# The first input tile alone at the head of SyncE's queue, one scaling piece on VectorE, and two small orders in layer 1

## The chip, the cores and the metric

The kernel runs on one core of a Trainium2 chip. The metric is the device time of one execution in microseconds; the median of several runs is compared. Five engines work side by side and meet through semaphores: TensorE (PE, with its weight loads PEld), VectorE (DVE), ScalarE (ACT), GpSimd (POOL) and SyncE (SP), which only issues transfers here. ACT and POOL issue transfers too; the queues of SP, ACT and POOL feed the same DMA engines.

## The reference

Two sequences of 512 tokens of width 1024 go through two layers and a final norm. Layer 0 mixes by a Fourier transform in 8 groups of 128 features, layer 1 by attention (8 heads, 2 key heads). Behind each stands a squared-ReLU MLP of width 4096. All is float32.

```python
def rms_norm(x, g):
    y = x32 * lax.rsqrt(jnp.mean(x32 * x32, axis=-1, keepdims=True) + EPS)
    return (y * g.astype(jnp.float32)).astype(x.dtype)

def fourier_mix(h, w_out):
    hg = h.astype(jnp.float32).reshape(B, S, N_FGROUPS, F_GROUP)
    f = jnp.fft.fft2(hg, axes=(1, 3), norm="ortho").real
    return f.reshape(B, S, D_MODEL) @ w_out

def sq_relu_mlp(h, w_up, w_down):
    a = jnp.maximum(h @ w_up, 0)
    return (a * a) @ w_down

for i in range(DEPTH):
    if i % N_MIXERS == 0:
        x = x + fourier_mix(rms_norm(x, fourier_norm[j]), fourier_w_out[j])
    else:
        x = x + gqa_attention(rms_norm(x, attn_norm[j]), ...)
    x = x + sq_relu_mlp(rms_norm(x, mlp_norm[i]), mlp_w_up[i], mlp_w_down[i])
return rms_norm(x, final_norm)
```

## The kernel before

**Numbers.** Nearly every float32 product is made of three products of halves: an operand is split into a high part (`split`: a cast on ACT, L86) and a low part (a subtraction on DVE, L87), and PE adds high x high, high x low and low x high in PSUM (`mm3`, `product`). The first transforms use plain float32.

**The head.** `begin()` starts the transfers. `g` is the Fourier norm's gain, 128 x 8 numbers (L377, on SP's queue). `load_x(0, t)` brings tile t of sequence 0, 128 tokens x 1024 (L352); tile 0 goes through ACT's queue, tiles 1 to 3 through SP's. `exact_table(4)`, `(5)` and `(6)` bring the tables of cosines and sines (L366, SP). SP's queue thus holds, in this order: g, tile 1, table 4, tiles 2 and 3, tables 5 and 6, and the Nyquist weights (L731). PE meanwhile runs `idle`, matmuls of 256 columns on a tile of ones, whose result nobody reads (L622): 12 of them, then 8 transposes that spread g over the partitions (L392), then 20 more.

All engines follow the written order here (`manual_schedule`). `f0 = Front(0, 0)` handles tiles 0 and 1. For each tile, ACT squares and sums (`squares`, L445) and POOL takes the inverse root (`root`, L449 and L450). Then, for tile 0, DVE multiplies by the gain in two halves, straight from the PSUM of g's transposes (`gain`, L459), adds the two halves (`plus`, L463) and subtracts them (`minus`, L472). `scale_both(0)` multiplies by the inverse root on ACT (L484) in four pieces: the sum's first 128 columns, its other 384, a short extract (128 x 40) for the Nyquist row, and the difference (128 x 512). The first piece is what the first matmul of the sequence transform reads (`exact_even`, L547), together with the first 258 columns of table 4. Then come `exact_nyq` (L554), which reads the extract, and `exact_odd` (L550), which reads the difference. Tile 1 goes the same way, and tiles 2 and 3 follow through `f1`, whose two tiles `combine` joins (L493 to L495).

**The MLP, first product.** The matrices are multiplied by a seven-product scheme on blocks of two by two. In `first_product` pairs of hidden blocks p = 0 to 15 run; for the first eight, the two products of a pair that go into its first row (`first`, `second`) come ahead of all others. `first` accumulates in a PSUM bank, and ACT copies the bank (L1081, `blocks.copied`). `second` goes on accumulating in the same bank, so it must wait for the copy. When it is done, ACT applies ReLU (L1062) and the square (L1063, `squared`). Here PE's order is in part written and in part the planner's; ACT's and DVE's order come from the planner, which takes `behind(x, y)` as an order between two instructions, without a wait. In layer 1, `behind(pairs[p - 1].squared, blocks.copied)` puts the square of one pair behind the copy of the next, for p from 4.

**The MLP, second product.** `second_product` walks over groups of 4, 4, 2 and 4 pairs in layer 1. For each group and each of four output columns m there is a step (`Sums`, five products) with a row (`Row`, two products) of the group that comes next. The row's first product is added to a common part on DVE (`add_e`, L1269, `r.added`). The operands were spilled to memory; `hook` brings the next group's back when it is time, and `put` splits each into two halves; `puts` holds their low parts. Where a step's rows have n = 2 and four low parts arose in the step, `behind(puts[1], rows[0].added)` puts the second low part behind the row's add. PE's order is written in this loop; the planner sets the others'.

Of the kernel before, what the change touches and what calls it, by code (L numbers as in the profile page):

```python
# [44 lines left out]
def trunk_kernel(ctx, tc, x_in, xt_in, y_out, tables, rope, gfour, gcol, grow, gfin,  # L45
# [298 lines left out]
    def load_x(q, t, queue=nc.sync):  # L344
        if (q, t) == (0, 0):
            wide = wp.tile([P, 2 * D], F32, tag="w", name=nm("w"))
            nc.vector.memset(wide[:, D : D + 1], (EPS * D) ** 0.5)
            xa[q, t] = wide[:, :D]
            xa[q, t, "eps"] = wide[:, : D + 1], wide[:, D + 4 :].bitcast(BF16)[:, : D + 1]
        else:  # L350
            xa[q, t] = slot([P, D], F32)
        return queue.dma_start(xa[q, t], x_in[q][t * P : (t + 1) * P, :])  # L352
# [8 lines left out]
        tabs[k] = slot([P, D], F32R)  # L361
        nc.gpsimd.dma_start(tabs[k][:, : tables[k].shape[-1]], tables[k])

    def exact_table(k):
        t = slot([P, D], F32)
        nc.sync.dma_start(t[:, : tables[k].shape[-1]], tables[k])  # L366
        exact.append(t)

    def w_pair(src, n, a):
        b = slot([P, D], F32)  # L370
# [3 lines left out]

    def begin():
        gr, g = slot([P, D], F32), cons.tile([P, KC], F32, name="g")
        nc.sync.dma_start(g, gfour)  # L377
        load_x(0, 0, nc.scalar)
        load_x(0, 1)
        exact_table(4)  # L380
        for t in range(2, 4):
            load_x(0, t)
        exact_table(5)
        exact_table(6)
        nc.scalar.preload_act_table_set("natural_log_exp_and_others")
        idle(ps(), 12)
        halves = []
        for i in range(2):
            o = ps()
            for k in range(4):  # L390
                c = 4 * i + k
                nc.tensor.transpose(o[:, k * P : (k + 1) * P], g[:, c : c + 1].broadcast_to([P, P]), ident)  # L392
            halves.append(o)
        return gr, halves
# [36 lines left out]
    class Front:  # L431
# [46 lines left out]
        def scale_both(self, i):  # L478
            if i == 0:
                self.n = exact[0][:, 772:852].rearrange("p (i a b) -> p i a b", i=2, a=5)  # L480
            p, m = self.p[i], self.m[i]
            first = ((p[:, :P], p[:, :P]), (p[:, P:], p[:, P:])) if i == 0 else ((p, p),)
            for out, x in first + ((self.n[:, i], eights(m)), (m, m)):
                nc.scalar.activation(out, x, AF.Copy, scale=self.r[:, i : i + 1])  # L484
                yield
            parts.append((self.p[i], self.m[i], self.n[:, i]))

# [131 lines left out]
    def idle(o, n):  # L619

        for _ in range(n):
            nc.tensor.matmul(o[:, :256], filler, filler.unsqueeze(1).broadcast_to([P, 2, P]), start=True, stop=True)  # L622
# [174 lines left out]
    with tc.manual_schedule(engines={ET.PE, ET.Activation, ET.DVE, ET.Pool, ET.SP}):  # L797
# [4 lines left out]
        ftX, pickX = exact[2][:, :256], exact[2][:, 256:334]  # L802
        f0, f1, wn = Front(0, 0), Front(0, 1), FoldNyq()
        wn.load()
        idle(ps(), 20)
        for i in range(2):
            f0.squares(i)
            f0.root(i)
# [244 lines left out]
    def first_product(l, blocks, rows, ahead, head=iter(())):  # L1053
# [122 lines left out]
        for p in range(AHEAD):  # L1176
            if p == late + 1:
                blocks.spread(1)
            pair = pairs[p]
            if p < len(rows):  # L1180
                pair.row = rows[p]
            else:
                pair.load()
                pair.split_row()
                if p < 6 and wo_added:
                    behind(pair.made[1], wo_added[0])
                if p == 4 and not l:
                    for x, y in zip(pair.made, blocks.r[1].made):
                        behind(x, y)
            with tc.manual_schedule(engines={ET.PE}) if p < 3 else nullcontext():  # L1190
                pair.first()
                if l and p > 3:
                    behind(pairs[p - 1].squared, blocks.copied)
                if p == 1:
                    blocks.split_sums(1)
                next(head, None)
                if p == 1:
                    pairs[0].second()
                if p == 2 == late:
                    blocks.root(1)  # L1200
                if p > 0:
                    pair.second()
                if p == 1 == late:
                    blocks.root(1)
            if p > 3:
                for _ in range(3):
                    next(todo)
            if p == 5:
                pairs[0].load_sums()
                pairs[0].sums_13()  # L1210
                pairs[0].sum_2()
            if p == 6:
                pairs[0].split_23()
# [36 lines left out]
    def second_product(l, blocks, rows, late=lambda: None, ready=lambda m: None, head=iter(())):  # L1250
# [214 lines left out]
        for k, (rows, sums) in enumerate(items):  # L1465
            nrows, nsums = items[k + 1] if k + 1 < len(items) else ([], None)
            end = sums.m if sums.g == len(GROUPS[l]) - 1 else -1
            if end in (0, 2):
                late()
            puts.clear()  # L1470
            with tc.manual_schedule(engines={ET.PE}):
                for r in rows:
                    r.first()
                    if r.m == 3:
                        change("b11", r.g)
                for r in nrows:
                    r.load()
                hook()
                for i, op in enumerate(("t1", "t3", "t2", "b22", "t4")):
                    sums.go(i)  # L1480
                    if sums.m == 3:
                        change(op, sums.g)
                    if i == 0 and nsums:
                        nsums.load()
                    if i == 1:
                        for r in rows:
                            r.second()
                            if r.m == 3:
                                change("b21", r.g)
                        if end == 1:  # L1490
                            late()
                            late()
                        hook()
                        for r in nrows:
                            r.split()
                    if i == 4 and nsums:
                        nsums.split_3()
                    hook()
                    if k == 0 and i in (2, 4):
                        change(ROW[i // 4], 0)  # L1500
                    if i == 2 and nsums:
                        x = nsums.sum_23()
                        if sums.n < nsums.n:
                            for r in rows:
                                behind(x[0], r.added)
                            for y in puts[2:]:
                                behind(y, x[1])
                        nsums.split_12()
                    if i == 3 and nsums:
                        nsums.sum_4()  # L1510
                        nsums.split_4()
            if rows and rows[0].n == 2 and len(puts) == 4:
                behind(puts[1], rows[0].added)
            for r in rows:
                finish(r.m)
            finish(sums.m)
# [728 lines left out]
```

## Time and profile before

| what | value |
|---|---|
| median of 3 runs | 1661.48 us (1661.46 to 1661.52) |
| the profiled execution | 1660.31 us |
| its span, first to last instruction | 1658.5 us |
| PE busy, matmuls | 1651.5 us, 7762 instructions |
| DVE, ACT, POOL busy | 1265.0, 878.3, 394.1 us |
| granted TensorE clock, mean | 0.999 |

The span is shorter than the execution by what lies around the first and the last instruction. Times in a timeline count from the span's start. A row of the timeline has start and duration in us, the engine, the line of the kernel, the operation, out<-in, and how many instructions were merged; brackets give the engine's idle time before it and what ended it. ACTq and SPq are the issuing parts of ACT and SP. A duration of merged matmuls reaches to the modelled end of the last one, so groups overlap a little.

### The profile page before, as it was taken

How to read it: one execution, taken by the hardware profiler on the slowest of the kernel's cores; microseconds unless marked ns; L12 is line 12 of the kernel's file. 1: busy time of each engine (PE TensorE's matmuls, PEld its weight loads, DVE VectorE, ACT ScalarE, POOL GpSimd, SP SyncE). 2: the span in 40 equal slices, each digit the busy share in tenths (PEclk: the TensorE clock that was granted, in tenths of full speed). 3: DMA queues.
4: the chain of work that ended last, by engine and by line, in shares of the span. 5: the costliest groups of instructions: out<-in, count | busy, mean ns of one | idle time of the engine just before them, and what ended most of it. 6: DMA issues, size and time to landing. Idle time of an engine off the chain costs nothing.

```text
span 1658.5 us, 22101 instructions
## 1 busy us (share of the span) xinstructions
PE 1651.5 (100%) x7762; PEld 1378.5 (83%) x7762; DVE 1265.0 (76%) x1797; ACT 878.3 (53%) x1551; POOL 394.1 (24%) x377
## 2 busy tenths in 40 slices
PE   9999999999999999999999999999999999999998
PEld 8988888888888888888888888888888888888887
DVE  8898785557886779868788888877855487878875
ACT  7776454446243425447688856554554552433335
POOL 5311443222000001325454303004422220000002
PEclk9999999999999999999999999999999999999999
DMA  9843554459775757425501146335544696756632
GB/s 313 241 172 108 196 210 165 146 193 371 229 237 172 246 180 228 177 66 199 166 1 39 65 175 231 127 108 180 201 149 168 226 366 200 233 163 221 186 114 103
DMA packets 121904, 301.43 MB, mean 182 GB/s; under 512 B 12312, under 2 KB 13720, under 8 KB 121792
## 3 DMA queue, kind: packets, MB, share of 16 engines
q1 hardware_dynamic: 98864, 253.66, 43.8%
q0 software_dynamic: 8528, 20.01, 5.7%
q10 hardware_dynamic: 14400, 26.35, 4.2%
q8 instruction: 61, 1.00, 0.2%
q14 instruction: 51, 0.42, 0.1%
HBM read 217.07 MB, written 82.38 MB: 181 GB/s over the span
## 4 chain that ended last, share of the span: by engine, by line
PE 98%; DVE 1%; issue 0%; ACT 0%; DMA 0%; POOL 0%; POOLq 0%; DVEq 0%; ACTq 0%
PE ps L1046 76%; PE ps L83 6%; PE ps L81 6%; PE ps L82 6%; PE ps L1657 2%; PE ps L1636 0%; PE ps L550 0%; PE ps L547 0%; DVE u L2002 0%; DMA g<-gfour 0%; PE ps L217 0%; PE ps L622 0%; PE ps L760 0%; PE ps L1626 0%; PE ps L587 0%
## 5 line engine op out<-in xcount | busy, mean ns | idle before, releaser
L1046 PE MATMUL ps<-u,w 128*128 128x512 f32 x4920 | 1124.6, 389 | 0.0
L1046 PEld LDWEIGHTS ps<-u,w 128*128 128x128 f32 x4920 | 922.7, 188 | 193.8 <-ACT u L1081 1.9
L86 ACT CAST w<-raw 128x1024 fp32r<-128x1024 f32 (+1 forms) x215 | 212.4, 993 | 309.6 <-PE ps L1046 235.9
L87 DVE TENSOR_TENSOR w<-raw,w 128x1024 fp32r<-128x1024 f32 (+1 forms) x215 | 249.3, 1164 | 66.6 <-ACT w L86 62.6
L86 ACT CAST u<-u 128x1024 fp32r<-128x1024 f32 (+1 forms) x140 | 140.7, 1046 | 84.9 <-PE ps L1046 37.4
L87 DVE TENSOR_TENSOR u<-u,u 128x1024 fp32r<-128x1024 f32 (+1 forms) x140 | 168.9, 1233 | 21.6 <-ACT u L86 20.7
L1046 PE MATMUL ps<-u,u 128*128 128x512 f32 x624 | 148.6, 389 | 0.0
L1296 POOL DMA_DIRECT2D raw<-w_sum x32 | 28.1, 879 | 468.5 <-DMA raw<-w_sum 167.6
L1166 POOL TENSOR_TENSOR u<-u 128x512 f32<-128x512 f32 x28 | 37.8, 1351 | 427.6 <-ACT u L1063 427.6
L1269 DVE TENSOR_TENSOR u<-ps,u 128x512 f32<-128x512 f32 x160 | 109.4, 685 | 36.8 <-PE ps L1046 34.0
L1046 PEld LDWEIGHTS ps<-u,u 128*128 128x128 f32 x624 | 117.1, 188 | 24.3
L81 PE MATMUL ps<-u,u 128*128 128x512 f32 (+2 forms) x342 | 129.0, 379 | 0.0
L83 PE MATMUL ps<-u,u 128*128 128x512 f32 (+2 forms) x342 | 124.5, 364 | 0.0
L82 PE MATMUL ps<-u,u 128*128 128x512 f32 (+2 forms) x342 | 124.2, 363 | 0.0
L177 POOL TENSOR_TENSOR t<-t,t 128x512 f32<-128x512 f32 (+1 forms) x47 | 67.5, 1441 | 187.2 <-ACT t L171 163.2
L1062 ACT ACTIVATE t<-t 128x512 f32<-128x512 f32 x64 | 40.5, 632 | 111.4 <-DVE t L1135 101.4
L87 DVE TENSOR_TENSOR u<-ps,u 128x512 fp32r<-128x512 f32 (+3 forms) x112 | 68.1, 635 | 7.3 <-ACT u L86 6.9
L83 PEld LDWEIGHTS ps<-u,u 128*128 128x128 f32 x342 | 64.3, 188 | 10.5 <-DVE u L87 0.4
L82 PEld LDWEIGHTS ps<-u,u 128*128 128x128 f32 x342 | 64.6, 189 | 8.5 <-DVE u L87 0.7
L81 PEld LDWEIGHTS ps<-u,u 128*128 128x128 f32 x342 | 64.7, 189 | 7.8
L1122 DVE TENSOR_TENSOR t<-ps,u 128x512 f32<-128x512 f32 x32 | 22.0, 687 | 60.9 <-PE ps L1046 50.3
L86 ACT CAST u<-ps 128x512 fp32r<-128x512 f32 (+3 forms) x112 | 59.4, 558 | 9.6 <-PE ps L1657 7.6
(270 smaller groups left out, 2013.3 us busy)
## 6 DMA issues: line engine op xcount, KB each, us to landing
raw<-w_up SPq DMA_DIRECT2D x80, 512.0 KB, 4.6
u<-spill_t SPq DMA_DIRECT2D x60, 512.0 KB, 7.0
raw<-w_sum SPq DMA_DIRECT2D x56, 512.0 KB, 5.6
u<-spill_b SPq DMA_DIRECT2D x45, 512.0 KB, 6.4
spill_t<-u SPq DMA_DIRECT2D x84, 256.0 KB, 2.0
spill_b<-t ACTq DMA_DIRECT2D x60, 256.0 KB, 4.2
raw<-w_row SPq DMA_DIRECT2D x28, 512.0 KB, 4.8
park<-u SPq DMA_DIRECT2D x24, 512.0 KB, 3.9
```

The source lines that it names most:

```text
L81: nc.tensor.matmul(out, lh, rh, start=first, stop=False)
L82: nc.tensor.matmul(out, lh, rl, start=False, stop=False)
L83: nc.tensor.matmul(out, ll, rh, start=False, stop=last)
L86: hi = nc.scalar.copy(dst_hi, src)
L87: return hi, eng.tensor_sub(dst_lo, src, f32(dst_hi))
L177: nc.gpsimd.tensor_add(acc[q][:, :n], acc[q][:, :n], s[:, :n])
L1046: nc.tensor.matmul(o, w[x][:, sl], h[k][y], start=first and k + i == 0, stop=k == n - 1 and i == 2, skip_group_check=not first)
L1062: nc.scalar.activation(t, src, AF.Relu)
L1166: eng.tensor_sub(t[:, 0], b12, b11)
L1269: return nc.vector.tensor_add(x, o, x)
L1296: nc.gpsimd.dma_start(s[:, 1], w[:, 3], accum_op=ALU.add)
L1657: nc.tensor.transpose(pt[:, t * P : (t + 1) * P], probs[t][:, sc * P : (sc + 1) * P], ident)
```

## The change

In the head, g moves to ACT's queue. Tile 0 moves to the head of SP's. Table 4 is brought in two transfers: its first 258 columns right behind tile 0, the rest behind tile 1. `exact_table` becomes a generator that issues one transfer at each step. The fillers ahead of the transposes go from 12 to 10, those behind them from 20 to 21. The first of tile 0's four scaling pieces moves from ACT to DVE, as a `tensor_scalar` with the same per-partition factor; the other pieces stay on ACT. In layer 1, the order of square and copy in the first product begins with pair 3 instead of 4. In the second product, all four low parts go behind the row's add, instead of the second one alone.

```diff
-    def exact_table(k):
+    def exact_table(k, cuts=()):
         t = slot([P, D], F32)
-        nc.sync.dma_start(t[:, : tables[k].shape[-1]], tables[k])
         exact.append(t)
+        edges = [0, *cuts, tables[k].shape[-1]]
+        for c0, c1 in zip(edges, edges[1:]):
+            nc.sync.dma_start(t[:, c0:c1], tables[k][:, c0:c1])
+            yield
...
-        nc.sync.dma_start(g, gfour)
-        load_x(0, 0, nc.scalar)
+        nc.scalar.dma_start(g, gfour)
+        load_x(0, 0)
+        pieces = exact_table(4, (258,))
+        next(pieces)
         load_x(0, 1)
-        exact_table(4)
+        for _ in pieces:
+            pass
         for t in range(2, 4):
             load_x(0, t)
-        exact_table(5)
-        exact_table(6)
+        for k in (5, 6):
+            for _ in exact_table(k):
+                pass
         nc.scalar.preload_act_table_set("natural_log_exp_and_others")
-        idle(ps(), 12)
+        idle(ps(), 10)
...
-            for out, x in first + ((self.n[:, i], eights(m)), (m, m)):
-                nc.scalar.activation(out, x, AF.Copy, scale=self.r[:, i : i + 1])
+            for j, (out, x) in enumerate(first + ((self.n[:, i], eights(m)), (m, m))):
+                if i == j == 0:
+                    nc.vector.tensor_scalar(out, x, self.r[:, :1], None, ALU.mult)
+                else:
+                    nc.scalar.activation(out, x, AF.Copy, scale=self.r[:, i : i + 1])
                 yield
...
-        idle(ps(), 20)
+        idle(ps(), 21)
...
-                if l and p > 3:
+                if l and p > 2:
                     behind(pairs[p - 1].squared, blocks.copied)
...
             if rows and rows[0].n == 2 and len(puts) == 4:
-                behind(puts[1], rows[0].added)
+                for y in puts:
+                    behind(y, rows[0].added)
```

## The prediction

> **What bounds the kernel now.** I read the page first, its busy shares and its chain of waits.
>
> ```profile
> span 1658.5 us, 22101 instructions
> PE 1651.5 (100%) x7762; PEld 1378.5 (83%) x7762; DVE 1265.0 (76%) x1797; ACT 878.3 (53%) x1551; POOL 394.1 (24%) x377
> PE 98%; DVE 1%; issue 0%; ACT 0%; DMA 0%; POOL 0%; POOLq 0%; DVEq 0%; ACTq 0%
> ```
>
> PE is busy for all but 7.0 of the 1658.5 us, and 98% of the chain is PE's own work. So an edit on another engine counts only where PE waits for it, and an edit of PE's own fillers counts directly, because PE has no later pause in which a late start could be made good. Next I read the timeline of the first 30 us, where most of the edits lie. Its columns are start, duration, engine, line, operation, and in brackets the idle time before it and what ended that.
>
> ```profile
> 0.72 0.41 ACTq L352 DMA_DIRECT2D w<-x  x1
> 0.73 0.39 SPq L377 DMA_DIRECT2D g<-gfour  x1
> 0.94 0.17 DVE L408 MEMSET u<- 128x128 f32 x1
> 1.16 2.93 PE L622 MATMUL ps<-u 128*128 128x256 f32 x12 [1.16 <-DVE w L347]
> 1.17 0.42 SPq L352 DMA_DIRECT2D u<-x  x1
> 4.32 1.23 PE L392 MATMUL ps<-ident,g 128*128 128x128 f32 x8 [0.23 <-DMA g<-gfour]
> 4.89 1.06 ACT L445 ACTIVATE w<-w 128x1025 bf16<-128x1025 f32 x1 [2.44 <-DMA w<-x]
> 5.16 1.28 DVE L459 TENSOR_TENSOR u<-w,ps 128x512 f32<-128x512 f32 x2 [3.99 <-PE ps L392]
> 5.31 2.64 PE L622 MATMUL ps<-u 128*128 128x256 f32 x20
> 6.12 1.06 ACT L445 ACTIVATE t<-u 128x1024 bf16<-128x1024 f32 x1
> 6.20 0.57 POOL L450 TENSOR_TENSOR s<-s,half 128x1 f32<-128x1 f32 x1 [3.72 <-ACT w L445]
> 6.47 0.69 DVE L463 TENSOR_TENSOR t<-u 128x512 f32<-128x512 f32 x1
> 7.08 0.68 DVE L472 TENSOR_TENSOR t<-u 128x512 f32<-128x512 f32 x1
> 7.26 0.91 ACT L484 ACTIVATE t<-t,s 128x128 f32<-128x128 f32 x2
> 7.79 2.00 PE L547 MATMUL ps<-u,t 128*128 128x257 f32 x8
> 8.46 0.72 ACT L484 ACTIVATE t<-t,s 128x512 f32<-128x512 f32 x1
> ...
> 16.25 0.81 DVE L495 SCALAR_TENSOR_TENSOR t<-t,s,t 128x512 f32<-128x512 f32 x1
> ...
> 17.51 0.59 PE L547 MATMUL ps<-u,t 128*128 128x257 f32 x2
> ```
>
> The reader is to see three strands that meet at 7.79, where the first real matmul (L547) begins. PE: 12 fillers, a 0.23 us wait for g, eight transposes of g, 20 fillers. DVE: it waits 3.99 us, not for the input tile but for the transposes (at 5.16), and then works through two gains, `plus` and `minus` without a pause. ACT: from 4.89 it squares tile 0, then tile 1, and only at 7.26 gets to the scaling piece that L547 reads. L547 starts when the last filler has been issued and the piece is ready, both at about the same time.
>
> **The change part by part: the head.** The fillers first. Twelve took 2.93 us, 0.244 each, so ten end at 1.16 + 2.44 = 3.60 instead of 4.09. The transposes cannot start before g has landed. g goes from SP's queue, issued at 0.73, to ACT's, issued at 0.72: 0.01 us apart. The next view is the DMA queues from 3.8 to 4.4 us (q10 is ACT's, q1 SP's).
>
> ```profile
> q10 hardware_dynamic: 50, 0.16, 65.6%
> q1 hardware_dynamic: 25, 0.09, 36.7%
> ```
>
> Here both queues are served side by side: while the last 0.16 MB of tile 0 move, 0.09 MB of SP's transfers move too. In front of SP's queue, with only g's 128 x 8 x 4 bytes beside it, tile 0 no longer shares this stretch. Two thirds of the engines' packets were its own, so some 0.2 of these 0.6 us are gained: it lands at 4.7 instead of 4.89. g stays one of two heads of queue issued at the same moment, so I take its landing as unchanged, with 0.2 us either way as a bound. The wait before the transposes then grows from 0.23 to 0.72 us: the two fillers taken away become idle time, and the transposes start at 4.32 as now. The added filler (2.64 / 20 = 0.13) has PE ready at 7.92 instead of 7.79.
>
> DVE is released by the transposes, so it starts at 5.16 as now, and an earlier tile 0 gives it nothing. `minus` ends at 7.76. Behind it comes the new operation, the 128x128 scaling. No DVE row shows this operation; the bounds are 0.17 (the 128x128 memset) and 0.41 (a two-input 128x256 pass, quoted below). I take 0.25, nearer the row of the same shape, and it ends at about 7.97, allowing 0.04 for the overlap that DVE's rows show (`minus` starts 0.08 before `plus` ends). L547 then starts at 8.0, **0.2 us later than now**.
>
> On ACT one piece goes away (two of them took 0.91). Against that, tile 1 now stands behind the first 258 columns of the table, 128 x 258 x 4 bytes = 0.13 MB, which is 0.3 us at the 0.25 MB in 0.6 us of the two rows above. The square of tile 1 moves from 6.12 to about 6.4, and the later scalings (the row at 8.46) end at about 9.3 instead of 9.18. They are read only after L547's eight matmuls, which end at 9.79 now and 0.2 later then, so this costs nothing; without that cover it would cost 0.1. What is late next is DVE, which has 0.25 us more in front of all its later work: at its end, the row at 16.25 finishes at 17.06 and L547 reads it at 17.51. The slack of 0.45 covers the 0.25, the more so as PE is later itself. The one added DMA issue (0.42 on SP) and tile 0's own move past g lie in front of transfers that stand in line anyway. The order of SP's bytes is otherwise as before, and the first part of the table lands sooner.
>
> The bounds of the head: if g landed by 3.60, PE would reach L547 at 3.60 + 0.99 (4.32 to 5.31) + 21 x 0.132 = 7.36, but DVE could not start before tile 0 at 4.7, and its chain of 2.6 us plus 0.25 gives 7.5: a gain of 0.3. If g landed 0.2 later, the loss would be 0.4.
>
> **The change in layer 1: the square.** The edit at line 1192 lets `behind` begin with pair 3 instead of pair 4. These are ACT's rows around pairs 3 and 4, then the weight loads' rows and their group of waits from 1040 to 1630 us.
>
> ```profile
> 1051.75 1.04 ACT L86 CAST w<-raw 128x1024 fp32r<-128x1024 f32 x1
> 1052.69 0.63 ACT L1063 ACTIVATE u<-u 128x512 f32<-128x512 f32 x1
> 1053.22 0.57 ACT L1081 COPY u<-ps 128x512 f32<-128x512 f32 x1
> ...
> 1057.44 1.04 ACT L86 CAST w<-raw 128x1024 fp32r<-128x1024 f32 x1
> 1058.53 0.59 ACT L1081 COPY u<-ps 128x512 f32<-128x512 f32 x1
> ```
>
> ```profile
> 1053.85 5.13 PEld L1046 LDWEIGHTS ps<-u,w 128*128 128x128 f32 x23 [0.33 <-ACT u L1081]
> 1059.17 0.99 PEld L1046 LDWEIGHTS ps<-u,w 128*128 128x128 f32 x5 [0.20 <-ACT u L1081]
> ```
>
> ```profile
> PEld ps L1046 <- ACT u L1081: 1.0, 4, 0.3
> ```
>
> PE accumulates pair 3's second product onto the bank that the copy (L1081) reads, so it waits for the copy. At pair 3 the square (L1063) stands between the cast and the copy; at pair 4 it does not. Put behind the copy, the square lets it start at 1052.69 instead of 1053.22, 0.53 earlier, which is more than the 0.33 that PE waited. The wait goes. Its worth is between 0 (if it hid behind matmuls in flight) and 0.33; I take **0.25 gained**, since such loads stand a little apart anyway. The square itself ends 0.5 later, in front of a store that nobody near awaits. Pair 4's 0.20 stays.
>
> **The four low parts.** The edit at line 1513 acts where a step's rows have n = 2 and four low parts are made: the step whose seven products of six matmuls end where PE's row at 1515.62 begins. At 0.227 us each (twelve from 1515.62 to 1518.34) these 42 take 9.5 us, so it starts at 1506.1. DVE's rows and PE's:
>
> ```profile
> 1505.28 1.22 DVE L87 TENSOR_TENSOR u<-u,u 128x1024 fp32r<-128x1024 f32 x1
> 1507.01 1.22 DVE L87 TENSOR_TENSOR u<-u,u 128x1024 fp32r<-128x1024 f32 x1
> 1508.74 0.68 DVE L1269 TENSOR_TENSOR t<-ps,t 128x512 f32<-128x512 f32 x1
> 1509.34 1.22 DVE L87 TENSOR_TENSOR u<-u,u 128x1024 fp32r<-128x1024 f32 x1
> 1511.07 1.21 DVE L87 TENSOR_TENSOR u<-u,u 128x1024 fp32r<-128x1024 f32 x1
> ...
> 1514.61 0.41 DVE L1344 TENSOR_TENSOR raw<-raw,raw 128x256 f32<-128x256 f32 x1
> ...
> 1517.61 0.68 DVE L87 TENSOR_TENSOR u<-raw,u 128x512 fp32r<-128x512 f32 x1
> ```
>
> ```profile
> 1515.62 2.88 PE L1046 MATMUL ps<-u,w 128*128 128x512 f32 x12
> 1518.34 2.88 PE L1046 MATMUL ps<-u,u 128*128 128x512 f32 x12
> ```
>
> Two low parts now run ahead of the row's add at 1508.74; afterwards all four run behind it. The row's product ends at 1506.1 + 6 x 0.227 = 1507.5, so the add can come at about 1507.7, and DVE stands idle for some 1.2 us before it. The lows follow from 1508.3, each with an add between, and end by about 1515. Their first reader is PE at 1515.62, which wants the second pair only one product and two sums later. Everything queued behind them moves by about 1.2 us: the low at 1517.61 would end at 1519.5 instead of 1518.29. It is read in the second product after 1518.34, six matmuls later (1519.7), at its third matmul (1520.2). The cover is 0.7 us. So the price is **0**, with bounds of 0 and about 0.5 if two more operations slip in front. It gains nothing either: the group of waits above holds nothing from this place.
>
> **The sum.** +0.2 - 0.25 + 0 = -0.05 us. The profiled execution took 1660.31 us, 1.81 around its span of 1658.5; the sum makes it 1660.26. The median of the runs, 1661.48, is 1.17 above the profiled one, so the forecast is **1661.4 us**, no change.
>
> **The rivals.** (1) *The clock stays low longer: slower.* The fillers went from 0.244 us each (the twelve) to 0.132 (the twenty): PE's pace doubles somewhere in the transposes, after some 3.5 us of nearly unbroken work. With 0.72 us of idle in that stretch instead of 0.23, the doubling may be refused. Then the 21 fillers cost up to 21 x 0.244 = 5.1 instead of 2.8, or, if the low pace lasts another 3.5 us, half of that is lost: +1.8, so 1663.2. It decides from the first such stretch; beyond 0.2% it takes two. For it speaks that idle time triples; against it that 0.23 did no harm and 80% of the stretch is still busy. [...]
>
> (2) *g lands earlier in ACT's queue.* Then the head gains up to 0.3 instead of losing 0.2, and with the square it is -0.55: 1660.9. For it: on ACT's queue g stands beside the tile from the first packet. Against: it did so on SP's.
>
> (3) *The low parts come too late.* DVE's idle 1.2 us is not caught up and PE waits at 1520: +0.5 to 1.2 on the forecast, 1662.2. For it: the first five DVE rows above alone take 5.6 of the 7.0 us from 1505.28 to 1512.28. Against: 0.7 us of cover.
>
> (4) *The layer-1 edits do not take hold*, because the planner finds another order for ACT and DVE: the head alone remains, 1661.7.
>
> **How the numbers follow.** The forecast 55%, (2) 22%, (4) 8%, (3) 7%, (1) 8%. The forecast's own bounds are 1661.1 to 1661.9. The range must reach to (2) and (4), and with (3) it is 1660.6 to 1662.4; (1) and odd ends stay outside. About 0.2%, 3.3 us, is what a measurement of this kernel can tell from no change: none of these cases reaches it. A gain of 3.3 us would need half of PE's whole idle time of 7.0 us, most of which lies before 1.16 and in the end part, where nothing is edited: faster 1%. Slower takes two refused doublings or a reordering that nothing here shows: 2%. Same 97%.
>
> **What would show it.** Head: the wait for g before L392 at about 0.7 us, L547 at about 8.0, a DVE row of 128x128 in front of it. If L392 starts before 4.1, (2) is right; if the second group of fillers runs at 0.24 us, (1). Layer 1: ACT's order cast, copy, square at 1052, and the 0.33 gone from the weight loads; four DVE lows behind the add, and no PE wait between 1515 and 1522. The forecast is wrong if the median moves by more than 1 us.

## The result, and the profile after

The changed kernel is **slower by about 2.3 us**: median 1663.57 us over 22 runs (1662.60 to 1664.47) against 1661.28 us over 22 runs of the kernel before (1660.42 to 1662.64) on the same chips. The ratio is 1.0014, with an interval of 1.0009 to 1.0020. The forecast was 1661.4, and its range ended at 1662.4.

The page of the profiled execution (1663.0 us; before 1660.31) has nearly the same busy shares as before (PE 99% after 100%), and PE is still nearly the whole chain. Its span is 2.7 us longer, and PE's busy time grew by only 1.3.

```profile
span 1661.2 us, 22097 instructions
PE 1652.8 (99%) x7761; PEld 1379.9 (83%) x7761; DVE 1266.4 (76%) x1798; ACT 878.5 (53%) x1550; POOL 394.2 (24%) x377
PE 97%; DVE 1%; DMA 1%; issue 0%; ACT 0%; POOL 0%; POOLq 0%; DVEq 0%; ACTq 0%
```

DMA's share of the chain rose from 0 to 1%. The waits of PE say where: columns are what waited, for whom, the sum in us, how often, and the longest.

```profile
PE ps L632 <- DVE w L347: 1.2, 1, 1.2
PE ps L399 <- DMA g<-gfour: 1.0, 1, 1.0
PE ps L1056 <- DVE w L87: 0.6, 1, 0.6
```

The first was there before. The wait for g (L399 is the old L392) was 0.23 and is 1.01. The third, for a low part of a weight, is new. These are the timeline rows of the first 18 us that answer to those of the kernel before (L632 is the old L622, L452 the old L445, L466 the old L459, L557 the old L547).

```profile
0.72 0.41 ACTq L380 DMA_DIRECT2D g<-gfour  x1
0.73 0.39 SPq L352 DMA_DIRECT2D w<-x  x1
...
1.16 2.50 PE L632 MATMUL ps<-u 128*128 128x256 f32 x10 [1.16 <-DVE w L347]
...
4.40 1.06 ACT L452 ACTIVATE w<-w 128x1025 bf16<-128x1025 f32 x1 [1.95 <-DMA w<-x]
...
4.67 1.94 PE L399 MATMUL ps<-ident,g 128*128 128x128 f32 x8 [1.01 <-DMA g<-gfour]
...
5.79 0.69 DVE L466 TENSOR_TENSOR u<-w,ps 128x512 f32<-128x512 f32 x1 [4.63 <-PE ps L399]
6.13 1.06 ACT L452 ACTIVATE t<-u 128x1024 bf16<-128x1024 f32 x1 [0.58 <-DMA u<-x]
...
6.26 3.86 PE L632 MATMUL ps<-u 128*128 128x256 f32 x21
...
8.61 0.27 DVE L492 TENSOR_SCALAR t<-t,s 128x128 f32<-128x128 f32 x1
...
9.96 1.90 PE L557 MATMUL ps<-u,t 128*128 128x257 f32 x8
```

Three things stand out. The transposes start at 4.67 instead of 4.32 and take 1.94 instead of 1.23. The 21 fillers behind them take 3.86, where 20 took 2.64. And the first real matmul starts at 9.96 instead of 7.79: 2.17 us later, where 0.2 was forecast. DVE's new piece ended at 8.88, 1.1 before that, so at the end PE waited for nothing but its own fillers.

**Where the 2.7 us of the span arose.** I counted the same matmul from the end of both kernels and took the difference of its start between the two profiled executions (the matmul records of the trace; missing ones filled in at the pace of their neighbours). "Head" is this lag at 700 us, "square" its change from 1040 to 1100, "low parts" from 1525 to 1560. The same was done for each experiment.

```
                        head   square  1100-1525  low parts   at 1640
after                   1.98   -0.24     0.02       0.92       2.74
e2_square_only          0.75   -0.21     0.17       0.00       0.72
e3_lows_only            0.30   -0.07     0.03       0.92       1.29
e4_fill16               1.17   -0.24     0.12       0.92       1.99
e5_fewer_fillers        2.39   -0.01    -0.01       0.00       2.43
e6_swap_queues          2.69   -0.03     0.48       0.00       3.11
e7_piece_dve            0.38   -0.02     0.13       0.01       0.48
e9_lows_order           0.25   -0.01     0.25       1.45       2.00
e12_lows_both           0.88   -0.10     0.54       0.54       1.82
e10_fill_14            -0.06   -0.21     0.03       0.18      -0.02
e11_g_first             0.08   -0.21     0.42       0.00       0.30
f2_g_first_again        0.10   -0.24     0.12       0.01      -0.02
f4_g_first_20          -0.07   -0.14     0.20       0.01       0.01
e13_best                0.15   -0.22     0.74       0.06       0.73
f1_after_g_sp           1.42   -0.16     0.29       0.92       2.47
f3_after_again          1.86   -0.20     0.03       0.95       2.64
```

For the changed kernel the ledger closes: +1.98 in the head, -0.24 for the square, +0.92 for the low parts. Two readings need care. The profiled execution of before (1660.31) was one of its quickest, about 1.0 under the median, so the head column overstates what a median loses. Lag that arose between about 20 and 700 us counts as head too: e11's lag is -0.18 at 20 us, and its 0.08 at 700 comes from a drift of 0.36 between 400 and 700 us for which I know no cause. And the stretch from 1100 to 1525 varies by up to 0.7 with no pattern among the edits.

One execution of e1_head_only, its profiled one, was disturbed (2068 us): its times stand without that one, and it has no row above.

### The profile page after: what moved, and what is told of

Its sections match the earlier page's. It is cut to its first block, busy times and chain, and to the rows that moved or that the text cites. A ratio compares the mean times of both kernels' runs of the same rounds, so it can differ in the third digit from the quotient of the medians.

```text
span 1661.2 us, 22097 instructions
## 1 busy us (share of the span) xinstructions
PE 1652.8 (99%) x7761; PEld 1379.9 (83%) x7761; DVE 1266.4 (76%) x1798; ACT 878.5 (53%) x1550; POOL 394.2 (24%) x377
## 4 chain that ended last, share of the span: by engine, by line
PE 97%; DVE 1%; DMA 1%; issue 0%; ACT 0%; POOL 0%; POOLq 0%; DVEq 0%; ACTq 0%
PE ps L1056 74%; PE ps L83 6%; PE ps L81 6%; PE ps L82 6%; PE ps L1668 2%; DMA u<-spill_t 1%; PE ps L1647 0%; PE ps L560 0%; PE ps L557 0%; DVE u L2013 0%; DVE u L87 0%; DMA g<-gfour 0%; PE ps L632 0%; PE ps L217 0%; DVE w L87 0%
```

## The experiments

Each was timed beside the kernel before on the same chip. Splitting table 4 was not run alone; in the changed kernel it shows no loss, since ACT squares tile 1 at 6.13 against 6.12 before. The theories to be told apart were three for the head: the two missing fillers leave PE idle, and the clock's doubling comes later; g lands later on ACT's queue; the piece on DVE is late. And one for layer 1: the low parts cost what the head does not.

**The parts alone.** e1 is the changed kernel without its layer-1 edits, e2 and e3 are the kernel before with one of them each.

```diff
 e1:  -                if l and p > 2:
      +                if l and p > 3:
      -                for y in puts:
      -                    behind(y, rows[0].added)
      +                behind(puts[1], rows[0].added)
 e2:  -                if l and p > 3:
      +                if l and p > 2:
 e3:  -                behind(puts[1], rows[0].added)
      +                for y in puts: behind(y, rows[0].added)
```

> The changed kernel's head on the old layer 1. Theory A (the clock): the head alone makes L557 start at 9.9 to 10.0 us, because the 21 fillers run at 0.21 us each up to about 8 us; the time is 1.7 to 2.2 us above the kernel before, and no wait of PE above 0.3 us is left after 1500 us. Theory B (the low parts): the head costs 0.2 to 1 us, as predicted or a little more, and the larger part of the 2.3 us is in layer 1.

> The kernel before, with the square behind the copy from pair 3 on and nothing else. Both theories: the 0.33 us that the weight loads waited at 1053.85 is gone, the waits for the copy fall from 1.9 to 1.6 us in total, and the time is 0.2 to 0.3 us below the kernel before, which is less than the runs scatter.

> The kernel before, with all four low parts behind the row's add and nothing else. If the wait of 0.8 us at 1547 us in the changed kernel comes from this edit: the same wait of 0.8 to 1.0 us on a low part of weights appears at about 1545 us, DVE stands idle for 2 us before an add at about 1530 us, and the span grows by about 0.9 us. If it comes from the head's shift against the transfers: no PE wait there, and the time is that of the kernel before.

Before, 31 runs: 1661.15. e1: nine runs, median 1662.71 (1661.80 to 1663.71), ratio 1.0008 [0.9998, 1.0018], **+1.6**, a little under the 1.7 to 2.2 expected. e2: 1660.80, ratio 0.9998 [0.9989, 1.0008], **-0.35**. e3: 1661.83, ratio 1.0005 [0.9996, 1.0015], **+0.7**. All three intervals hold 1. For e1 the runs still lie apart: its lowest is above 26 of the 31 of before. For e2 and e3 the medians alone would not settle it; the ledger does, with -0.14 to -0.24 in all ten kernels with the square's edit against -0.10 to -0.01 in the six without, and 0.92 to 0.95 in all five with the plain low-part edit against 0.18 at most in the nine without any. The medians add up to 1.6 - 0.35 + 0.7 = 1.9 of the 2.3 measured.

**The clock.** e4 gives the changed kernel 16 fillers ahead of the transposes, so that PE is busy until g is there. e5 does the opposite to the kernel before: two fillers fewer, and nothing else.

```diff
 e4 (from after):   -        idle(ps(), 10)
                    +        idle(ps(), 16)
 e5 (from before):  -        idle(ps(), 12)
                    +        idle(ps(), 10)
```

> The changed kernel with 16 fillers instead of 10 ahead of the transposes, so that PE does not stand idle until g lands at about 4.7 us. Theory A: the clock rises at about 4.7 us again, the second group of fillers runs at 0.12 us each, L557 starts at 8.4 to 8.8 us, bound by the piece on DVE, and the time falls by 1.0 to 1.5 us against the changed kernel, in spite of six fillers more. Theory B (idle time has nothing to do with it): the six fillers delay the transposes by some 0.1 us and the time stays or grows.

> The kernel before with 10 fillers ahead of the transposes instead of 12, all else as before. [...]

e4: 1662.26 (before 1661.15; ratio 1.0008 [0.9998, 1.0017]), so **1.3 faster than the changed kernel with six more fillers to run**, or 1.2 when each is taken against its own runs of before (+1.1 and +2.3). e5: 1662.65 (before 1661.43; 1.0008 [0.9998, 1.0017]), **+1.2 for taking work away**. The intervals hold 1, but all ten runs of e4 lie below the median of the changed kernel, and all ten of e5 above 29 of the 31 of before. PE's rows of the first 11 us, e4 first, then e5:

```profile
4.75 1.94 PE L399 MATMUL ps<-ident,g 128*128 128x128 f32 x8
6.34 2.96 PE L632 MATMUL ps<-u 128*128 128x256 f32 x21
```

```profile
4.41 1.94 PE L392 MATMUL ps<-ident,g 128*128 128x128 f32 x8 [0.75 <-DMA g<-gfour]
6.00 4.51 PE L622 MATMUL ps<-u 128*128 128x256 f32 x20
```

In e4 no idle time stands before the transposes and 21 fillers take 2.96; in e5, after 0.75 us of idle, 20 take 4.51. The counts of PE instructions in one-microsecond windows show the change of pace (the second number of PE's pair, in brackets; instructions that reach in from a neighbouring window are counted too, so the counts are above the true rate); first the changed kernel, then the kernel before.

```profile
7.00:8.00 1.00, 1.00 (x7) 1.00 (x6) 0.97 (x2) 0.28 (x2) 0.56 (x2) 1.00 1.04 426
8.00:9.00 1.00, 1.00 (x7) 1.00 (x7) 1.00 (x4) 0.82 (x2) 0.50 (x1) 1.00 0.99 397
9.00:10.00 1.00, 1.00 (x11) 1.00 (x10) 1.00 (x2) 0.97 (x3) 0.00 (x0) 1.00 1.05 414
```

```profile
5.00:6.00 1.00, 1.00 (x12) 1.00 (x10) 0.84 (x2) 1.00 (x2) 0.00 (x0) 1.00 1.02 414
6.00:7.00 1.00, 1.00 (x11) 1.00 (x10) 0.96 (x2) 0.92 (x2) 0.57 (x1) 1.00 1.03 420
```

The count is seven until about 9 us, then eleven; before, it is eleven or twelve from 5 us on. (The column of the granted clock reads 1.00 throughout and does not show this step; the matmuls do.) The trace also records the moment of the step. Beside it, the idle time just before the transposes:

```
clock doubles at (us)   idle before the transposes (us)
e10 4.06  e3 4.12  e7 4.12     0.35  0.69  0.60
e11 4.34  f4 4.49              none  none
before 4.69  e9 4.91           0.23  0.52
f2 6.00  f1 6.13  e2 6.31      none  none  0.51
e12 6.51  e4 6.80  e13 7.10    0.43  none  none
f3 8.24  after 8.77            1.11  1.01
e6 10.08  e5 10.24             1.04  0.75
```

The four executions with 0.75 us or more ahead of the transposes have their step at 8.24 or later, the thirteen others by 7.10. In e10, e3 and e7 it came at 4.06, 4.12 and 4.12, just as their idle time began (4.08 to 4.09). That idle time moves the step is shown by e4 (none, and the step at 6.80; the changed kernel 1.01 and 8.77) and e5 (0.75 and 10.24; the kernel before 0.23 and 4.69), one execution of each, with the medians behind them. How it does so these runs do not show, and among the thirteen the step still lies anywhere from 4.06 to 7.10.

**What makes the idle time.** e6 swaps only the queues of g and tile 0 in the kernel before. e7 puts only the first scaling piece on DVE.

```diff
 e6:  -        nc.sync.dma_start(g, gfour)
      -        load_x(0, 0, nc.scalar)
      +        nc.scalar.dma_start(g, gfour)
      +        load_x(0, 0)
 e7:  -            for out, x in first + ((self.n[:, i], eights(m)), (m, m)):
      -                nc.scalar.activation(out, x, AF.Copy, scale=self.r[:, i : i + 1])
      +            for j, (out, x) in enumerate(first + ((self.n[:, i], eights(m)), (m, m))):
      +                if i == j == 0:
      +                    nc.vector.tensor_scalar(out, x, self.r[:, :1], None, ALU.mult)
      +                else:
      +                    nc.scalar.activation(out, x, AF.Copy, scale=self.r[:, i : i + 1])
```

> The kernel before with g on ACT's queue and tile 0 at the head of SP's, all else as before (12 and 20 fillers, tile 1 directly behind tile 0, table 4 whole). If ACT's queue makes g late: the transposes start at 4.7 us or later, 0.1 to 0.5 us later than in the kernel before (4.3 to 4.8 in four executions), PE's idle time passes 0.6 us in part of the executions, and the time grows by 0.2 to 0.8 us. If the queue does not matter: transposes at 4.3 to 4.8, tile 0 read at 4.4 to 4.6 instead of 4.9 to 5.2, time within 0.2 us.

> The kernel before with the first scaling piece on DVE, all else as before. By the prediction's step the piece takes 0.25 us behind the difference and makes the first real matmul 0.2 us later where the clock is up early; where the clock comes late the fillers set the start and it costs nothing. The median grows by 0.0 to 0.2 us.

e6: 1663.26 (before 1661.18), **+2.1**, ratio 1.0008 [0.9999, 1.0017], far more than the 0.2 to 0.8 expected. e7: 1661.36, ratio 1.0001 [0.9992, 1.0010], no difference that the runs can tell: the piece is not the cause. PE's rows of e6:

```profile
5.12 1.94 PE L392 MATMUL ps<-ident,g 128*128 128x128 f32 x8 [1.04 <-DMA g<-gfour]
6.72 4.13 PE L622 MATMUL ps<-u 128*128 128x256 f32 x20
```

With all 12 fillers there, g alone makes PE idle for 1.04. So the swap does it alone, and the two fillers do it alone. Their losses (2.1 and 1.2) do not add up in the changed kernel's head (1.6); this fits that all three lose the same thing, an early step: it came at 10.08 in e6, at 10.24 in e5 and at 8.77 in the changed kernel, against 4.69 before. The queues show why g is late. Here are the packets of the kernel before from 1.6 to 2.1 us (number, MB, share of the engines), and those of the changed kernel in the same stretch, then from 2.6 to 3.1, then from 3.9 to 4.2.

```profile
q10 hardware_dynamic: 5, 0.02, 30.9%
q1 hardware_dynamic: 32, 0.00, 2.9%
```

```profile
q1 hardware_dynamic: 15, 0.06, 57.1%
...
q1 hardware_dynamic: 36, 0.15, 74.3%
q10 hardware_dynamic: 36, 0.00, 3.6%
...
q1 hardware_dynamic: 110, 0.13, 120.8%
q10 hardware_dynamic: 6, 0.00, 1.1%
```

On SP's queue (q1, before), g's packets of 32 bytes flow from 1.6 us on. On ACT's queue (q10, after) not one has been sent by 2.1; they begin after that, go one for one with tile 0's packets of 4 KB, and the last ones lie behind 3.9. Where this wait bounds the transposes, they start at 4.32 to 4.77 with g on SP's queue (eight executions, mean 4.54) and at 4.67 to 5.12 with g on ACT's (three, mean 4.85): 0.3 later in the mean, though the ranges overlap. In both orders g shares the engines with tile 0.

**g ahead of tile 0 on one queue.** If the sharing is what delays g, both on SP's queue with g first should bring it early. e11 does this in the kernel before, with the square's edit and 14 fillers instead of 20; e10 is its control, without the move; f2 is e11 again, f4 keeps 20 fillers. f1 puts g back at the head of SP's queue in the changed kernel, with tile 0 behind it; f3 is the changed kernel again.

```diff
 e10, e11, f2:   -        idle(ps(), 20)
                 +        idle(ps(), 14)
 e11, f2, f4:    -        load_x(0, 0, nc.scalar)
                 +        load_x(0, 0)
 e10, e11, f2, f4:  -                if l and p > 3:
                    +                if l and p > 2:
 f1 (from after):   -        nc.scalar.dma_start(g, gfour)
                    +        nc.sync.dma_start(g, gfour)
```

> The kernel before with the square's edit and 14 fillers instead of 20 behind the transposes. Under theory A the clock comes late in a part of the executions whatever the kernel does, and then 20 fillers at 0.21 us delay the first real matmul, which waits for them and not for its operand: six fewer save up to 1.3 us in those executions and nothing in the others, so the median falls by 0.3 to 0.8 us below the kernel before, 0.25 of it from the square. If the fillers are needed to bring the clock up: the time grows by up to 1 us.

> As the run before this one (square, 14 fillers), with tile 0 behind g on SP's queue, ahead of tile 1, and nothing on ACT's queue. If g lands at 4.2 to 4.9 us because it takes turns with tile 0's packets: it now lands before 4.0, the transposes start at 4.1 with no wait for g, and the first real matmul comes 0.2 to 0.6 us earlier than in the run before. If its landing is the transfers' own start-up time: it lands as before and nothing changes, or tile 0 lands 0.1 to 0.2 us later.

> The changed kernel with g back on SP's queue, ahead of tile 0, and nothing else altered. If g's place is what makes the head late: g lands before 4.0 us, PE stands idle for less than 0.5 us ahead of the transposes, the clock is up by 7.5 us at the latest, and the time is 1.2 to 1.8 us below the changed kernel, about 1662. If the two fillers fewer or the split table do it: the time stays above 1663.

> The run with g first, 14 fillers and the square's edit again: 1660.2 to 1661.0 us in every execution, 0.7 to 1.0 us below the kernel before by the medians.

> The changed kernel once more. [...]

> The same with 20 fillers behind the transposes, as in the kernel before. If g's landing makes the gain: 1660.4 to 1661, like the run with 14. If it is the six fillers: it scatters up to 1662 like the kernel before, 0.3 to 0.6 us above the run with 14.

All beside a median of 1661.43 of before: e10 1661.07, ratio 0.9999 [0.9990, 1.0009]; e11 **1660.42** (1660.16 to 1660.97), 0.9996 [0.9986, 1.0005]; f2 **1660.34** (11 runs, 1660.16 to 1661.30), 0.9994 [0.9986, 1.0003]; f4 1660.67, 0.9995 [0.9986, 1.0004]. f3 1663.65, as the changed kernel before it. f1 1662.58, 1.0009 [0.9999, 1.0018]: 1.1 better than the changed kernel, a little short of what was expected, and still 1.15 behind before. Rows of e11, its q1 from 1.6 to 2.1 us first:

```profile
q1 hardware_dynamic: 144, 0.00, 14.3%
```

```profile
3.88 1.26 PE L392 MATMUL ps<-ident,g 128*128 128x128 f32 x8
...
4.82 1.06 ACT L445 ACTIVATE w<-w 128x1025 bf16<-128x1025 f32 x1 [2.82 <-DMA w<-x]
...
4.90 1.91 PE L622 MATMUL ps<-u 128*128 128x256 f32 x14
...
7.53 2.07 PE L547 MATMUL ps<-u,t 128*128 128x257 f32 x8 [0.73 <-ACT t L484]
```

All of g is sent by 2.1 us, the transposes follow the twelve fillers without a pause at 3.88, and tile 0, now behind g, lands no later than before (4.82 against 4.89). PE now waits 0.73 for ACT: fillers are no longer what sets the start. The gain over the median of before is about 1 us, some 0.3 of it the square's; against its control e10, the move itself gained 0.65. Each interval alone still holds 1, but all 21 runs end by 1661.30, below the median of before. It fits that the start no longer depends on when the clock's step comes: those 21 runs spread over 1.1 us, those of before in the same two batches over some 3. The clock's step came at 4.34 in e11's profiled execution and at 6.00 in f2's, and their heads are 0.08 and 0.10. f4 lies 0.33 above f2, less than these runs can tell, so what the six fillers add stays open.

In f1 there is no idle time either, yet L557's row breaks:

```profile
3.46 1.91 PE L399 MATMUL ps<-ident,g 128*128 128x128 f32 x8
...
7.97 1.06 ACT L452 ACTIVATE t<-u 128x1024 bf16<-128x1024 f32 x1 [1.94 <-DMA u<-x]
8.12 0.60 PE L557 MATMUL ps<-u,t 128*128 128x257 f32 x2
...
9.67 1.57 PE L557 MATMUL ps<-u,t 128*128 128x257 f32 x6 [0.96 <-ACT t L494]
```

Tile 1, behind the first 258 columns of the table, came only at 7.97; ACT squares it before it scales tile 0's other pieces, so PE stood again for 0.96. From 4.0 to 8.2 us the transfers moved 293 GB/s here, against 416 in the changed kernel and 415 in e11. This is one execution; the time of its packets came to 0.95 of the engines' time there, against 1.04 and 1.02, so a byte took about 1.3 times as long. Why is open.

**The low parts.** In the changed kernel a new wait of PE stands at 1548.57, its DVE rows ahead of it:

```profile
1532.57 0.69 DVE L1279 TENSOR_TENSOR t<-ps,t 128x512 f32<-128x512 f32 x1 [2.03 <-PE ps L1056]
...
1547.29 1.22 DVE L87 TENSOR_TENSOR w<-raw,w 128x1024 fp32r<-128x1024 f32 x1
...
1548.57 11.63 PE L1056 MATMUL ps<-u,w 128*128 128x512 f32 x50 [0.62 <-DVE w L87]
```

The kernel before had at these places:

```profile
1528.67 2.35 DVE L87 TENSOR_TENSOR u<-u,u 128x1024 fp32r<-128x1024 f32 x2
1530.94 0.68 DVE L1269 TENSOR_TENSOR t<-ps,t 128x512 f32<-128x512 f32 x1
...
1543.99 1.22 DVE L87 TENSOR_TENSOR w<-raw,w 128x1024 fp32r<-128x1024 f32 x1
```

Before, DVE filled the time ahead of the add with two low parts of 2.35 us. Given the new order, the planner put them behind the add in a **later** step than the one the edit names (the rows there belong to the group of 4, and the edit acts on those with n = 2), DVE stood for 2.03 us, and the weight's low part came 3.3 us later (1.5 of it beyond the 1.8 by which PE itself was late there). e9 and e12 are e3 with more orders written out, to bring those low parts back ahead: e9 ahead of the row's add alone, e12 ahead of the step's first sum too.

```diff
 e9:   +                            for y in puts[:2]: behind(rows[0].added, y)
 e12:  -                    add(dst, self.o[bank])
       +                    x = add(dst, self.o[bank]); self.made = x if i == 0 else self.made
       +                            [behind(z, y) for y in puts[:2] for z in (rows[0].added, sums.made)]
```

> The low parts' edit alone, and besides two low parts of the next but one step ordered ahead of that step's row add, as they stood in the kernel before. If the wait at 1546 us comes from DVE standing idle for 2.0 us before that add, with low parts queued behind it: the idle time and PE's wait of 0.89 us are gone, and the time is that of the kernel before within 0.3 us. If it comes from the four low parts themselves moving later: the wait stays at 0.5 to 0.9 us.

> The low parts' edit alone, with both low parts of the later step ordered ahead of that step's row add and ahead of its first product's add, which restores DVE's order of the kernel before around 1529 us. If PE's wait of 0.89 us at 1546 us came from DVE standing idle there with the low parts queued behind the add: no wait above 0.3 us of PE between 1500 and 1560 us, and a time within 0.3 us of the kernel before. If the four low parts' own delay at 1508 us does it: the wait stays.

e9 missed: 1663.22 (before 1661.43; 1.0010 [1.0000, 1.0019]), slower than e3. Its DVE rows and its wait of PE:

```profile
1529.22 1.22 DVE L87 TENSOR_TENSOR u<-u,u 128x1024 fp32r<-128x1024 f32 x1
1532.69 0.69 DVE L1269 TENSOR_TENSOR u<-ps,u 128x512 f32<-128x512 f32 x1 [2.25 <-PE ps L1046]
1533.30 1.22 DVE L87 TENSOR_TENSOR u<-u,u 128x1024 fp32r<-128x1024 f32 x1
```

```profile
PE ps L1046 <- DVE t L1269: 1.2, 1, 1.2
```

The planner slid another add, which itself waited 2.25 for PE, between the two low parts, and the wait moved to the place of the row's add. With that way out closed, e12 came to 1661.47 (before 1661.18, 1.0001 [0.9992, 1.0010]):

```profile
1530.44 2.58 DVE L87 TENSOR_TENSOR u<-u,u 128x1024 fp32r<-128x1024 f32 x2 [0.40 <-ACT u L86]
```

```profile
PE ps L1046 <- DVE w L87: 0.2, 1, 0.2
```

With the pair back ahead of the add, the loss at this place fell from 0.92 to 0.54 (the ledger). So the reordering explains some four tenths of it. The rest may be the delay that the four low parts themselves pass down DVE's line, or the later landing of the operands; that stays open.

**A version of all that held.** e13 has g first, 12 fillers on both sides, the square, and the piece on DVE between `plus` and `minus` instead of behind them.

```diff
 e13:  -        load_x(0, 0, nc.scalar)
       +        load_x(0, 0)
       -            first = ((p[:, :P], p[:, :P]), (p[:, P:], p[:, P:])) if i == 0 else ((p, p),)
       +            first = ((p[:, P:], p[:, P:]),) if i == 0 else ((p, p),)
       -        idle(ps(), 20)
       +        idle(ps(), 12)
       +        nc.vector.tensor_scalar(f0.p[0][:, :P], f0.p[0][:, :P], f0.r[:, :1], None, ALU.mult)
       -                if l and p > 3:
       +                if l and p > 2:
```

> g and behind it tile 0 at the head of SP's queue, 12 fillers on either side of the transposes, the square's edit, and the first scaling piece on DVE between the sum and the difference instead of behind both. The piece is then ready at 7.0 to 7.1 us, where the run with g first waited for ACT until 7.5: the first real matmul starts at 7.1 to 7.2, and the time is 0.2 to 0.4 us below that run, 1.1 to 1.5 below the kernel before. If the idle time ahead of the first real matmul now holds the clock back: the time scatters up to 1662 again.

1660.98 (11 runs, before 1661.18), 0.9996 [0.9987, 1.0005]: not better than e11. The piece was ready at 7.64, not at the 7.0 to 7.1 expected, so the first real matmul started at 7.70, and this execution lost 0.74 between 1100 and 1525, as e6 and e12, which share none of its edits beyond tile 0's queue (e6), lost 0.5. The best version seen is e11: g ahead of tile 0 on SP's queue, the square, and 14 fillers.

## Why the prediction was wrong, by its own steps

**"I take its landing as unchanged, with 0.2 us either way as a bound": this step failed first.** The issue times agreed (0.72 and 0.73) and I let them stand for the landing. On ACT's queue the transposes that wait for g started 0.3 later in the mean, and in e6 0.8 after the 4.32 of before, beyond the bound. The wait before the transposes was 1.01 instead of 0.72.

**Rival (1), the clock, given 8%, is what happened.** The text named the idle time, the place, and the sign to look for ("if the second group of fillers runs at 0.24 us"), and 21 fillers took 3.86 us, 0.18 each, at the slow pace for about two thirds of that time (6.26 to 8.77). The low pace lasted 4.1 us longer than in the profiled execution of before (8.77 against 4.69), where the text had "another 3.5 us". Its price of 1.8 over the forecast stands against 1.6 for the head alone in e1. That its 1663.2 lies so near the 1663.57 measured is in part luck: the low parts and the square, which it leaves out, come to +0.35 together. The step that failed is the weighing, "against it that 0.23 did no harm and 80% of the stretch is still busy": 0.23 said nothing of 0.72, and one execution in which the step fell early (4.69) served as the kernel's usual pace. "PE ready at 7.92" rested on that.

**"So the price is 0" for the low parts failed.** Rival (3) was right in kind and wrong in place: PE waited at 1548, not at 1520. I followed the edited step's own queue, which did keep its cover. DVE stood idle there for 1.36 us, close to the 1.2 that I had allowed, though ahead of another low part that waited for ACT, and the row's add came behind it:

```profile
1510.18 0.69 DVE L87 TENSOR_TENSOR u<-raw,u 128x512 fp32r<-128x512 f32 x1 [1.36 <-ACT u L86]
1510.79 0.68 DVE L1279 TENSOR_TENSOR t<-ps,t 128x512 f32<-128x512 f32 x1
```

All four low parts stood behind the add, as forecast, and PE had no wait between 1515 and 1522. They were later than I had reckoned: in e3, which has this edit alone, the add came at 1509.12 instead of 1507.7 and the last of the four ended at 1516.74 instead of 1515. But the edit is an order given to a planner, and the planner changed a step 25 us later. Measured: 0.9 us in the trace, 0.7 in medians; within that rival's "+0.5 to 1.2", though at a place that its reason did not cover.

**The square was right**: ACT's order after is cast, copy, square.

```profile
1053.76 1.04 ACT L86 CAST w<-raw 128x1024 fp32r<-128x1024 f32 x1
1054.85 0.59 ACT L1091 COPY u<-ps 128x512 f32<-128x512 f32 x1
1055.34 0.63 ACT L1073 ACTIVATE u<-u 128x512 f32<-128x512 f32 x1
```

The ledger has -0.24 against the -0.25 predicted. Right too were the piece on DVE (0.27 against 0.25) and that tile 0 lands earlier (4.40; I had 4.7). This earliness bought nothing, as said: DVE waits for the transposes. Tile 1's square came at 6.13 instead of 6.4. Rivals (2) and (4) did not happen in the changed kernel; but once g stands alone at the front of a queue, something like the gain that (2) hoped for is there: in e11 the first real matmul starts at 7.53 instead of 7.79, and at 20 us 0.18 is left of it. The rest of e11's gain in the medians fits executions in which the clock comes late.

The sum was -0.05. With the measured terms it is +1.6 (head, e1) - 0.35 (e2) + 0.7 (e3) = +1.9, and 2.3 was measured; the 0.4 left is within what these medians can tell.

## What to carry to other kernels

What follows is drawn from this one kernel. A few fillers at the start are not a cost to be trimmed by their own duration: where they bridge the wait for the first data, the idle time that replaces them can put off the doubling of the clock (two fillers fewer in e5: 0.75 us of idle time instead of 0.23, and the step at 10.24 us instead of 4.69), so count idle time between the first matmul and the clock's step, and not in one execution alone. A small transfer that the first work needs is best put alone ahead of the large ones on the same queue; beside a large one on another queue it shared the engines packet by packet (36 packets of each from 2.6 to 3.1 us), and the transposes waited for it until 4.67 us, where with it alone in front they start at 3.88 without a wait (e11). An order given to a planner is to be priced over the whole loop that it plans: compare an engine's full sequence before and after, not the edited step.

## What the runs showed of the hardware that I had not expected

- Taking two idle-time matmuls away cost 1.2 us (e5), and adding six won 1.3 (e4).
- The step to the doubled clock came anywhere from 4.06 to 10.24 us: at 8.24 or later in the four profiled executions with 0.75 us or more of idle time ahead of the transposes, by 7.10 in the thirteen others. Whether most of the scatter of the kernel before (1660.42 to 1662.64) comes from the step is not shown: that kernel has one profile.
- With issues 0.01 us apart, the first packets on ACT's queue went out after 2.1 us where SP's had begun before that, when SP's queue carried the large tile. The two queues shared the engines, in the changed kernel with 36 packets of each from 2.6 to 3.1 us; but the choice of queue also moved the start of the transposes that wait for these 4 KB by 0.3 us in the mean (4.85 against 4.54), and with it the clock (step at 10.08 us in e6).
- f1's transfers ran at 293 GB/s from 4.0 to 8.2 us where the changed kernel, with the same bytes in line, had 416; no run here says why.
